# Modulation steps of a decoder trunk's first layer: smaller first blocks, shift and scale side by side, x loaded behind the first steps, and another cost model under the scheduler

## The chip, the cores and the metric

The kernel runs on one core of a Trainium2 chip. The metric is the device time of one execution in microseconds. The kernel before takes 2581.92 us, the median of three runs (2581.72 to 2582.03). The engines named below are TensorE (PE in the profile, its weight loads PEld), VectorE (DVE), ScalarE (ACT), GpSimd (POOL) and SyncE (SP), which issues the kernel's DMAs.

## The reference, cut to what matters

Two layers, 256 tokens, width 2048, FFN width 5632, all in f32:

```python
c_act = silu(c)
for l in range(2):
    mod = c_act @ w_mod[l] + b_mod[l]                  # 2048 x 12288 weights
    shift1, scale1, gate1, shift2, scale2, gate2 = split(mod, 6)
    h = rms_norm(x, norm1_gain[l]) * (1 + scale1) + shift1
    x = x + gate1 * mixer(h, ...)                      # in-projection, three mixers, w_out
    h = rms_norm(x, norm2_gain[l]) * (1 + scale2) + shift2
    x = x + gate2 * (silu(h @ w_gate[l]) * (h @ w_up[l])) @ w_down[l]
return rms_norm(x, final_norm_gain)
```

The mixer projects h with `w_in`, gives its column groups to three token mixers (A: gated linear attention, B: sliding-window attention with rotary positions, C: gated delta rule), concatenates their outputs and projects them with `w_out`. No output of a layer can start before its modulation (`mod`) is there, and `mod` reads 100 MB of weights per layer for a single vector.

## The kernel before, in words

Rows of x are two blocks of 128; the contraction of every projection runs over 16 K tiles of 128. `stream` (from L293) loads one K tile of up to 1024 columns (L323), multiplies it with both row blocks (L358) and gives the finished sums to an evacuation. A weight tile is used either "whole", in one f32 pass, or split into a high part (`wh`, ACT, L330) and a low part (`wl`, DVE, L331) for three faster passes. Layer 0's in-projection and out-projection are whole, all else but a few tiles is split. Loaded tiles live in nine slots (`raw`, `wh`, `wl`).

The modulation is not done on TensorE. `mod_segment` loads rows of `w_mod` (L220) and DVE adds each, times one number of silu(c) per partition, to an accumulator (L223): one **step**. After the 16 K tiles of a segment, `finish` folds the 128 partitions: for shift and scale by four transposes on TensorE (L248) and a sum on DVE (L250, L253, L256), for gates by a product with ones (L238). Layer 0's shift1 and scale1 are cut by K block (`K_BLOCKS`, L37): 512 columns a step, one DMA of 128x512, tiles `g` from an 18-buffer pool. All later segments are 1024 wide, tiles `mraw`, whose pool has two buffers, accumulators `acc`, also two. A queue `mods` holds the steps in the order in which they are wanted; `tick` issues some after each weight tile, by a rate for each stage.

Layer 0's in-projection goes block by block through K: norm the block's columns of x with the shift and scale of that block (L441 to L451), project the groups `qk`, `z`, `v` and `bq` over the block's K tiles, and add the sums to those of earlier blocks on DVE (L969); the first block is copied on ACT (L967). Behind the last block come the keys of B and the delta rule of C (levels at L678, L685 and the transpose L403), then B (L895, L911, L916), the in-projection of A, A itself (L823), the out-projection, norm2 and the FFN. Layer 1 runs the same with one block of all 16 K tiles.

The order in which these calls are written is not the order of the instructions. The framework's scheduler, entered with `tile.TileContext` (L1214), takes the whole program and sets each engine's order by its cost model, keeping the dependences; buffers are then given in that order. SP issues nearly all the kernel's DMAs in one order, and an issue that waits for its buffer holds up all those behind it.

The two places in the code before around the change that the listing does not explain by itself: `K_BLOCKS` is read at L475 to build `mods` and in `layer` to build the blocks, and layer 0 squares x for its norm (L1042) right after it is loaded.

## Time and profile before

| | us |
|---|---|
| median of the runs | 2581.92 |
| profiled execution | 2585.34 |
| its span, first to last instruction | 2583.5 |
| first product of the in-projection | 40.83 |
| last step of the first K block's modulation | 34.92 |

All in all the core moves 600.79 MB at a mean of 233 GB/s; 320 loads of `mraw` are 512 KB each, 128 loads of `g` are 256 KB. The mean granted clock of TensorE is 0.986. In the views below, a window's row gives the stretch, its length, the busy microseconds of PE, PEld, DVE, ACT and POOL with the number of instructions, the granted clock as a share of full speed, the busy share of the 16 DMA engines, and GB/s. A row of the chain gives a start, a duration, the engine and the operation that the end waited for at that time; "issue" is time in which the engine waited for nothing that the profile shows. The page's fifth part and "by line" rows give shares of the span by what the chain was made of.

### The profile page before, as it was taken

The numbers are of one execution on the slowest core, as the hardware profiler recorded it, in microseconds if no ns is written. First come the engines' busy times: TensorE is split into PE (matmuls) and PEld (weight loads), VectorE is DVE, ScalarE is ACT, GpSimd is POOL, SyncE is SP. The second block draws the span as 40 slices with busy tenths as digits, with TensorE's granted clock in tenths as the row PEclk, the third lists the DMA queues.
The fourth block names the chain that finished last, engine by engine and source line by source line (L and its number), as shares of the span: only waits on it lengthen the run. The fifth ranks groups of instructions, "written<-read, shape, count | busy, mean of one in ns | idle before, by whom it ended". The sixth has DMA issues, their size and how long they took to land.

```text
span 2583.5 us, 30803 instructions
## 1 busy us (share of the span) xinstructions
PE 2432.7 (94%) x11164; PEld 1884.1 (73%) x11164; DVE 1714.4 (66%) x2171; ACT 1053.5 (41%) x1548; POOL 58.2 (2%) x117
## 2 busy tenths in 40 slices
PE   4999998889999988999999999999999999999998
PEld 2555785447878767788877878877778878888876
DVE  6767867576675777657578785888664575544555
ACT  2203443124444333344335454564644434344443
POOL 1000000000000000000000000000000000000000
PEclk9999999989999999999999999999999999999999
DMA  9996538777778888868687861675676686666654
GB/s 341 368 322 204 180 114 282 258 231 268 261 259 260 283 268 274 292 193 286 223 277 261 281 192 50 214 232 192 212 256 193 200 286 195 188 191 188 189 184 155
DMA packets 190033, 600.79 MB, mean 233 GB/s; under 512 B 21628, under 2 KB 26268, under 8 KB 189496
## 3 DMA queue, kind: packets, MB, share of 16 engines
q1 hardware_dynamic: 189880, 598.81, 70.7%
q8 instruction: 88, 1.44, 0.2%
q14 instruction: 65, 0.53, 0.1%
HBM read 596.63 MB, written 2.10 MB: 232 GB/s over the span
## 4 chain that ended last, share of the span: by engine, by line
PE 57%; DMA 20%; DVE 10%; issue 8%; ACT 4%; POOL 1%; SPq 1%; DVEq 0%; ACTq 0%; POOLq 0%
PE acc L358 48%; DMA mraw<-in_w_mod 13%; DVE wl L331 4%; DMA raw<-in_w_down 3%; DMA raw<-in_w_in 2%; DVE acc L223 2%; ACT wh L330 1%; PE mm L403 1%; PE ga L895 1%; DMA raw<-in_w_up 1%; PE mm L678 1%; PE mm L685 1%; PE ga L916 1%; DMA raw<-in_w_gate 1%; PE fin L248 1%
## 5 line engine op out<-in xcount | busy, mean ns | idle before, releaser
L358 PE MATMUL acc<-wh,hm 128*128 128x512 f32 (+3 forms) x4872 | 1339.2, 389 | 20.9 <-DVE xs L931 4.7
L330 ACT ACTIVATE wh<-raw 128x1024 fp32r<-128x1024 f32 (+3 forms) x669 | 684.7, 1025 | 985.8 <-PE acc L358 548.9
L331 DVE TENSOR_TENSOR wl<-raw,wh 128x1024 fp32r<-128x1024 f32 (+3 forms) x669 | 785.2, 1179 | 446.6 <-ACT wh L330 444.5
L358 PEld LDWEIGHTS acc<-wh,hm 128*128 128x128 f32 x4872 | 892.0, 189 | 215.8 <-issue 25.5
L358 PE MATMUL acc<-wl,hm 128*128 128x512 f32 (+3 forms) x2484 | 792.3, 394 | 12.2 <-DVE wl L331 9.7
L223 DVE SCALAR_TENSOR_TENSOR acc<-mraw,c_act,acc 128x1024 f32<-128x1024 f32 x320 | 410.3, 1282 | 225.2 <-DMA mraw<-in_w_mod 222.9
L358 PEld LDWEIGHTS acc<-wl,hm 128*128 128x128 f32 x2484 | 458.4, 190 | 124.1 <-DVE wl L331 22.3
L358 PE MATMUL acc<-wh,ahl 128*128 128x512 f32 x560 | 158.4, 397 | 0.0
L358 PEld LDWEIGHTS acc<-wh,ahl 128*128 128x128 f32 x560 | 105.8, 189 | 24.5
L358 PE MATMUL acc<-wl,ahl 128*128 128x512 f32 x280 | 90.8, 398 | 7.2 <-DVE wl L331 7.2
L223 DVE SCALAR_TENSOR_TENSOR g<-g,c_act,g 128x512 f32<-128x512 f32 x128 | 88.7, 747 | 12.6 <-DMA g<-in_w_mod 12.4
L358 PE MATMUL acc<-wh,b 128*128 128x512 f32 (+2 forms) x184 | 74.7, 545 | 2.2 <-ACT b L447 2.1
L358 PE MATMUL acc<-wl,b 128*128 128x512 f32 (+2 forms) x176 | 67.1, 518 | 2.6 <-DVE g L969 2.6
L358 PEld LDWEIGHTS acc<-wl,ahl 128*128 128x128 f32 x280 | 52.2, 189 | 23.1 <-DVE wl L331 11.3
L358 PE MATMUL acc<-raw,b 128*128 128x512 f32 (+2 forms) x176 | 67.6, 524 | 0.0
L358 PEld LDWEIGHTS acc<-wh,b 128*128 128x128 f32 x184 | 35.2, 197 | 30.8 <-issue 23.1
L358 PEld LDWEIGHTS acc<-wl,b 128*128 128x128 f32 x176 | 32.8, 192 | 29.2 <-issue 20.3
L416 ACT ACTIVATE acc<-xs 128x512 f32<-128x512 f32 x32 | 19.0, 595 | 85.7 <-DVE xs L931 85.7
L447 ACT ACTIVATE b<-mm,mod,mod 128x128 f32<-128x128 f32 x24 | 9.2, 461 | 109.7 <-DVE mod L256 92.1
L358 PEld LDWEIGHTS acc<-raw,b 128*128 128x128 f32 x176 | 33.5, 195 | 26.7 <-issue 21.7
L929 DVE TENSOR_TENSOR acc<-acc,gate 128x512 f32<-128x512 f32 x64 | 43.0, 695 | 10.3 <-PE acc L358 10.2
L358 PE MATMUL acc<-raw,hm 128*128 128x512 f32 x88 | 41.7, 598 | 1.4 <-ACT acc L416 1.4
(314 smaller groups left out, 1645.8 us busy)
## 6 DMA issues: line engine op xcount, KB each, us to landing
mraw<-in_w_mod SPq DMA_DIRECT2D x320, 512.0 KB
raw<-in_w_down SPq DMA_DIRECT2D x176, 512.0 KB
raw<-in_w_gate SPq DMA_DIRECT2D x160, 512.0 KB
raw<-in_w_up SPq DMA_DIRECT2D x160, 512.0 KB
raw<-in_w_in SPq DMA_DIRECT2D x72, 512.0 KB
g<-in_w_mod SPq DMA_DIRECT2D x128, 256.0 KB
raw<-in_w_out SPq DMA_DIRECT2D x43, 512.0 KB
raw<-in_w_in SPq DMA_DIRECT2D x32, 264.0 KB
```

The lines of the kernel that those rows point to most:

```text
L223: V.scalar_tensor_tensor(acc, raw[:, a], c_act[:, i + a:i + a + 1], acc, ALU.mult, ALU.add)
L248: TE.transpose(ps[:, i * P:(i + 1) * P], acc[:, (j + i) * P:(j + i + 1) * P], ident)
L330: A.activation(wh[:, :width], raw[:, :width], AF.Copy)
L331: V.tensor_tensor(wl[:, :width], raw[:, :width], wh[:, :width].bitcast(F32), ALU.subtract)
L358: TE.matmul(ps[blk, j][:, :segs[j][2]], xa, parts[j][part], start=i == 0 and n == 0, stop=last and n == len(terms) - 1)
L403: TE.transpose(ps[:, j * P:(j + 1) * P], src[:, j * P:(j + 1) * P], ident)
L416: A.activation(scr[0]() if junk is None else junk, xs[:, blk, j * 512:(j + 1) * 512], AF.Square, accum_out=ssq[blk][:, j:j + 1])
L678: TE.matmul(ps[:, s], LT[blk][:, s], Tm[blk][:, s], start=True, stop=True)
L685: TE.matmul(ps[:, s], U[blk][:, s], m1[:, s], start=True, stop=True)
L895: TE.matmul(ps[:, j * nk:(j + 1) * nk], qT[rows, i + j], kT[rows, g, :nk], start=True, stop=True)
L916: TE.matmul(ps[:, j * 64:(j + 1) * 64], pT[:, j * nk + kb * P:j * nk + (kb + 1) * P], kv[kb][:, P + g * 64:P + (g + 1) * 64], start=kb == ...
L929: V.tensor_tensor(ps, ps, need(gate_row, (l, part, j)), ALU.mult)
```

## The change

It has five parts. `K_BLOCKS` becomes (2, 2, 4, 4, 4). For the two blocks of two K tiles, `first_segment` puts the shift columns and the scale columns side by side: one DMA of 128x2x256, one step, one fold of four transposes for both. x is loaded by row block, each half after four modulation steps, and the constants and norm gains after that (they came first). The small per-layer vectors and the rotary tables move behind the `qk`, `z` and `v` products of the first block. And the scheduler's context is opened with `schedule_with_timeline_sim=True`, so that it ranks instructions by a finer model of the engines; that reorders every engine's instructions from the first to the last.

```diff
--- before.py
+++ after.py
@@ -34,7 +34,7 @@
 FAR = 1.0e30
 
 
-K_BLOCKS = (4, 4, 4, 4)
+K_BLOCKS = (2, 2, 4, 4, 4)
 TAIL_OUT = (3, 6)
 TAIL_FFN = (3, 5)
 LEAD_FFN = (0, 0)
@@ -148,7 +148,6 @@
 
 
     ct = tl(kp, [P, N_FULL], "consts")
-    SY.dma_start(ct, consts[:, :N_FULL])
     n_mask = CONSTS.shape[1] - N_FULL
     masks = tl(kp, [P, n_mask], "masks", BF16)
     c_raw = tl(kp, [P, KD], "c_raw")
@@ -171,32 +170,69 @@
     c_act = tl(kp, [P, KD], "c_act")
     A.activation(c_act, c_raw, AF.Silu)
 
-
...
     trig = {}
...
-    SY.dma_start(xs, x.rearrange("(b p) d -> p b d", p=P))
+
+    def rotary():
+
+        pos_i = tl(kp, [P, NB], "pos_i", I32)
+        SY.dma_start(pos_i, pos)
...
+            trig[name] = r
 
 
     mod_col, gate_row = {}, {}
     SHIFT1, SCALE1, GATE1, SHIFT2, SCALE2, GATE2 = range(6)
+
+    def first_segment(k0):
+
+
+        width = 2 * P
+        st = {}
+
+        def mods_at(w):
+            return w[:, :2 * D].rearrange("p (s n) -> p s n", s=2)[:, :, k0 * P:k0 * P + width]
+
+        def step(i):
+            if i == 0:
+                st["acc"] = scr[1]()
+                G.memset(st["acc"], 0.0)
+                SY.dma_start(st["acc"][0:1].rearrange("p (s n) -> p s n", s=2),
+                             mods_at(b_mod[0:1]))
+            acc = st["acc"]
+            raw = scr[1]()
+            SY.dma_start(raw.rearrange("p (s n) -> p s n", s=2),
+                         mods_at(w_mod[0, i * P:(i + 1) * P]))
+            V.scalar_tensor_tensor(acc, raw, c_act[:, i:i + 1], acc, ALU.mult, ALU.add)
+            if i + 1 == KD:
+                fins.append([FIN_LAG, lambda: finish(acc)])
+
+        def finish(acc):
+            t = tl(smp, [P, 4], f"modfirst{k0}")
+            ps = tl(psf, [P, 512], "fin")
+            for i in range(4):
+                TE.transpose(ps[:, i * P:(i + 1) * P], acc[:, i * P:(i + 1) * P], ident)
+            V.tensor_reduce(t, ps.rearrange("p (a b) -> p a b", a=4), AX.X, ALU.add)
+            V.scalar_tensor_tensor(t[:, 2:], t[:, 2:], 1.0, gains[:, 0, k0:k0 + 2],
+                                   ALU.add, ALU.mult)
+            for j in range(2):
+                mod_col[0, SHIFT1, k0 + j] = t[:, j:j + 1]
+                mod_col[0, SCALE1, k0 + j] = t[:, 2 + j:3 + j]
+
+        return [((0, SHIFT1), lambda i=i: step(i)) for i in range(KD)]
 
     def mod_segment(l, part, k0, nk):
 
@@ -459,7 +495,6 @@
 
     small_t, wgk_t = {}, {}
     gains = tl(kp, [P, DEPTH, 2 * KD], "gains")
-    SY.dma_start(gains, small[:, :, :2 * KD].rearrange("l p n -> p l n"))
 
     def load_small(l):
         small_t[l] = tl(kp, [P, SMALL_W], "small")
@@ -473,8 +508,11 @@
 
     k0 = 0
     for n in K_BLOCKS:
-        for pair in zip(*(mod_segment(0, part, k0, n) for part in (SHIFT1, SCALE1))):
-            mods.extend(pair)
+        if n == 2:
+            mods.extend(first_segment(k0))
+        else:
+            for pair in zip(*(mod_segment(0, part, k0, n) for part in (SHIFT1, SCALE1))):
+                mods.extend(pair)
         k0 += n
     for l in range(DEPTH):
         for parts in ((GATE1,), (SHIFT2, SCALE2), (GATE2,)) if l == 0 else (
@@ -948,7 +986,8 @@
 
     def layer(l):
         wi, wo = w_in[l], w_out[l]
-        load_small(l)
+        if l:
+            load_small(l)
         blocks, at = [], 0
         for n in (K_BLOCKS if l == 0 else (KD,)):
             blocks.append(range(at, at + n))
@@ -1036,6 +1075,14 @@
             gemm(segs, ks, lhs, land(first, last, at), whole=ks if WHOLE_IN[l] else (),
                  lead=ahead(*LEAD_IN) if l and name == "qk" else ())
 
+        if l == 0:
+
+            for blk in range(NB):
+                for _ in range(4):
+                    mods.popleft()[1]()
+                SY.dma_start(xs[:, blk], x[blk * P:(blk + 1) * P])
+            SY.dma_start(ct, consts[:, :N_FULL])
+            SY.dma_start(gains, small[:, :, :2 * KD].rearrange("l p n -> p l n"))
         for blk in range(NB):
             if l == 0:
                 for j in range(4):
@@ -1051,6 +1098,8 @@
             for name in ("qk", "z", "v"):
                 project(name)
             if l == 0 and first:
+                load_small(l)
+                rotary()
                 for o in range(0, n_mask, 512):
                     n = min(512, n_mask - o)
                     t = scr[1]()
@@ -1211,7 +1260,7 @@
         args.append(nc.dram_tensor(f"in_{n}", a.shape, mybir.dt.from_np(a.dtype),
                                    kind="ExternalInput").ap())
     args.append(nc.dram_tensor("out_0", (T, D), F32, kind="ExternalOutput").ap())
-    with tile.TileContext(nc) as tc:
+    with tile.TileContext(nc, schedule_with_timeline_sim=True) as tc:
         trunk(tc, *args)
     r = run_bass_kernel_spmd(nc, [named], core_ids=[0])
     return r.results[0]["out_0"].reshape(1, T, D)
```

The moves, at three places. First SP's order while the second K block's and third K block's modulation is loaded (`g` on a 128x2x256 or 128x512 shape: steps of layer 0's shift and scale; `mraw`: 1024-wide steps, here of gate1; `wh`, `wl`, `raw` from in_w_in: in-projection tiles). Before, at the start of the second block:

```order
L323 DMA wh_347<-in_w_in 128x1024
L213 DMA g_357<-in_b_mod 1x512
L220 DMA g_360<-in_w_mod 128x512
L213 DMA g_363<-in_b_mod 1x512
L220 DMA g_366<-in_w_mod 128x512
L220 DMA g_369<-in_w_mod 128x512
L323 DMA wl_372<-in_w_in 128x1024
L220 DMA g_378<-in_w_mod 128x512
L220 DMA g_381<-in_w_mod 128x512
```

and after the change, in the second block and into the third:

```order
L217 DMA g_281<-in_w_mod 128x2x256
L249 DMA acc_1274<-in_b_mod 1x1024
L256 DMA mraw_1277<-in_w_mod 128x1024
L256 DMA mraw_1286<-in_w_mod 128x1024
L217 DMA g_284<-in_w_mod 128x2x256
```

```order
L256 DMA g_423<-in_w_mod 128x512
L359 DMA wl_566<-in_w_in 128x512
L359 DMA wl_566<-in_w_in 128x256
L359 DMA raw_586<-in_w_in 128x1024
L256 DMA mraw_1311<-in_w_mod 128x1024
L256 DMA mraw_1314<-in_w_mod 128x1024
L256 DMA g_429<-in_w_mod 128x512
L249 DMA g_426<-in_b_mod 1x512
L256 DMA g_442<-in_w_mod 128x512
```

Loads of gate1 rows now stand among the steps of shift and scale, where before none did. Counting bytes down SP's order: the last step of the first block stands at 10.9 MB before and at 8.1 after; of the later blocks, after, at 19.4, 37.0, 52.8 and 64.8.

Second, TensorE's order in layer 0's delta rule (L403, L678 and L685 before are L439, L716 and L723 after; 128x512 rows are products of projections, `ga` rows belong to attention, `fin` to a fold). Before:

```order
L403 MATMUL mm_1713<-consts_88,g_1650 128x128 x4
L678 MATMUL mm_1719<-g_1693,g_1681 128x128 x4
L358 MATMUL acc_2497<-wh_2608,hm_993 128x512
L358 MATMUL acc_2498<-wh_2608,hm_993 128x512
L358 MATMUL acc_2493<-wh_2629,hm_657 128x512
L358 MATMUL acc_2494<-wh_2629,hm_657 128x512
L358 MATMUL acc_2493<-wl_2630,hm_657 128x512
L685 MATMUL mm_1726<-g_1724,g_1690 128x128 x4
L358 MATMUL acc_2494<-wl_2630,hm_657 128x512
```

After:

```order
L954 MATMUL ga_2290<-kv_349,b_2283 128x64
L954 MATMUL ga_2290<-kv_354,b_2283 128x64
L723 MATMUL mm_1769<-g_1767,g_1733 128x128 x4
L933 MATMUL ga_2298<-kT_1468,b_2213 128x256 x2
L439 MATMUL mm_1775<-consts_88,g_1736 128x128 x4
L716 MATMUL mm_1781<-g_1693,g_1681 128x128 x4
L723 MATMUL mm_1788<-g_1786,g_1690 128x128 x4
L949 MATMUL ga_2309<-consts_88,b_2296 128x128 x4
L284 MATMUL fin_3646<-consts_88,acc_3476 128x128 x4
L439 MATMUL mm_1794<-consts_88,g_1693 128x128 x4
L716 MATMUL mm_1800<-g_1736,g_1724 128x128 x4
```

```order
L439 MATMUL mm_1813<-consts_88,g_1736 128x128 x4
L716 MATMUL mm_1819<-g_1693,g_1681 128x128 x4
L439 MATMUL ga_2338<-consts_88,b_120 128x128 x4
L394 MATMUL acc_3457<-wl_3451,hm_1429 128x512
L394 MATMUL acc_3458<-wl_3451,hm_1429 128x512
L394 MATMUL acc_3457<-raw_3467,hm_1429 128x512
```

Before, projection products stand one to four at a time between the steps of each level; after, a level's steps follow one another with attention's between, and the products come in groups of eight.

Third, SP's order where layer 1's in-projection begins. Before:

```order
L220 DMA mraw_11475<-in_w_mod 128x1024
L323 DMA raw_9772<-in_w_in 128x1024
L323 DMA raw_9793<-in_w_in 128x1024
L220 DMA mraw_11514<-in_w_mod 128x1024
L323 DMA raw_9814<-in_w_in 128x1024
L323 DMA raw_9832<-in_w_in 128x1024
L213 DMA acc_11472<-in_b_mod 1x1024
L213 DMA acc_12251<-in_b_mod 1x1024
L220 DMA mraw_11550<-in_w_mod 128x1024
L220 DMA mraw_11571<-in_w_mod 128x1024
L220 DMA mraw_11592<-in_w_mod 128x1024
```

After:

```order
L359 DMA raw_9541<-in_w_down 128x1024
L359 DMA raw_9766<-in_w_in 128x1024
L359 DMA raw_9794<-in_w_in 128x1024
L359 DMA raw_9815<-in_w_in 128x1024
L359 DMA raw_9836<-in_w_in 128x1024
L359 DMA raw_9857<-in_w_in 128x1024
```

Layer 1's in-projection tiles are no longer interleaved with `mraw` loads: from the first in_w_in load of layer 1 to its last in_w_out load there are 64 of these before and none after.

33 lines of the change are left out of this document (15 added, 18 removed).

## The prediction

> **What bounds the kernel now.** I read the engine totals and the chain of the page first, then the first 90 us and the end of layer 0's mixers as a chain of waits in order of time, then the stages as windows.
>
> ```profile
> PE 2432.7 (94%) x11164; PEld 1884.1 (73%) x11164; DVE 1714.4 (66%) x2171; ACT 1053.5 (41%) x1548; POOL 58.2 (2%) x117
> ...
> PE 57%; DMA 20%; DVE 10%; issue 8%; ACT 4%; POOL 1%; SPq 1%; DVEq 0%; ACTq 0%; POOLq 0%
> PE acc L358 48%; DMA mraw<-in_w_mod 13%; DVE wl L331 4%; DMA raw<-in_w_down 3%; DMA raw<-in_w_in 2%; DVE acc L223 2%; ACT wh L330 1%; PE mm L403 1%; PE ga L895 1%; DMA raw<-in_w_up 1%; PE mm L678 1%; PE mm L685 1%; PE ga L916 1%; DMA raw<-in_w_gate 1%; PE fin L248 1%
> ```
>
> TensorE is busy for 2432.7 of 2583.5 us, so 151 us are idle, and no instruction of TensorE goes or comes with this change. It can win back idle time (and a lowered clock behind it) or add some. The largest part of the chain that isn't TensorE is the stream of modulation weights, 13%. Where the idle time lies:
>
> ```profile
> 40.00:220.00 180.00, 175.81 (x529) 97.47 (x530) 125.86 (x218) 29.25 (x66) 2.73 (x16) 0.99 0.95 336
> ...
> 220.00:400.00 180.00, 173.51 (x1032) 137.21 (x1030) 136.71 (x269) 83.98 (x193) 11.72 (x17) 0.96 0.51 160
> 400.00:590.00 190.00, 164.23 (x595) 87.97 (x594) 127.98 (x178) 52.95 (x117) 8.66 (x9) 0.94 0.74 243
> 590.00:980.00 390.00, 373.28 (x1635) 300.04 (x1634) 268.45 (x243) 155.45 (x164) 2.86 (x3) 1.00 0.82 273
> 980.00:1370.00 390.00, 373.69 (x1637) 300.76 (x1636) 260.75 (x254) 156.43 (x175) 4.39 (x6) 0.99 0.78 257
> 1370.00:1600.00 230.00, 221.11 (x1289) 186.10 (x1288) 173.09 (x291) 117.90 (x207) 6.30 (x21) 0.99 0.63 202
> 1600.00:1840.00 240.00, 223.61 (x1240) 180.06 (x1240) 186.61 (x279) 135.69 (x270) 13.91 (x17) 0.98 0.59 190
> 1840.00:2583.00 743.00, 724.07 (x3206) 592.36 (x3204) 408.18 (x387) 310.68 (x336) 1.08 (x2) 0.99 0.65 207
> ```
>
> Columns are stretch, length, busy PE, PEld, DVE, ACT, POOL, clock, DMA share, GB/s. The first 40 us are nearly all idle; the K loop (40 to 220) loses 4; layer 0's mixers 6.5 and then 25.8, with the clock at 0.96 and 0.94 (another 7 + 11 us of full speed); layer 0's FFN 33; layer 1's mixers 8.9 + 16.4, and about 7 by the clock; the rest 19.
>
> **Part 1, the head.** How fast weights arrive, and what the first product waits for:
>
> ```profile
> 0.00:10.00 10.00, 0.00 (x0) 0.00 (x0) 2.18 (x16) 4.69 (x7) 3.59 (x23) 1.00 0.78 267
> 10.00:20.00 10.00, 1.11 (x4) 0.71 (x4) 6.43 (x14) 6.50 (x18) 1.95 (x2) 1.00 0.92 310
> 20.00:30.00 10.00, 0.00 (x0) 0.00 (x0) 9.62 (x15) 0.00 (x0) 0.00 (x0) 1.00 0.99 349
> 30.00:40.00 10.00, 2.23 (x8) 1.43 (x8) 8.51 (x14) 0.00 (x0) 1.05 (x2) 1.00 1.01 372
> ...
> 40.00:80.00 40.00, 39.17 (x115) 22.32 (x116) 27.82 (x45) 10.06 (x24) 1.27 (x2) 1.00 1.02 375
> 80.00:120.00 40.00, 39.22 (x130) 22.10 (x129) 30.75 (x55) 6.22 (x15) 1.46 (x14) 1.00 1.01 361
> ```
>
> ```profile
> 34.92 0.76 DVE g L223
> 35.72 1.13 PE fin L248 x4
> 36.88 0.70 DVE sums L250
> 37.62 1.13 PE fin L248 x4
> ...
> 40.83 2.08 PE acc L358 x2
> ```
>
> By these rates 2.7 MB have come by 10 us, 5.8 by 20, 9.3 by 30, 13.0 by 40, 28.0 by 80. In the order before, 10.9 MB stand up to the 32nd modulation step: 34.3 us by the rates, and the row has its last step at 34.92. So the queue's bytes date the head well. From that step to the first product pass 5.2 us (35.68 to 40.83), with two folds; one fold in place of two saves one pair of rows, 1.8 us, so I take 3.4.
>
> After the change, counted down SP's order in bytes: the last of the 16 side-by-side steps of block 0 stands at 8.1 MB, which is 26.7 us; with the step's 0.7 and the fold's 3.4 the first product starts at 30.8, **10 us earlier**. But a block of two K tiles covers half the time. Sixteen K tiles take 180 us (the window 40 to 220), 11.2 each, so block 0's products end at 53.2. Block 1's last step stands at 19.4 MB, and 13.0 MB at 40 us plus 6.4 at 375 GB/s is 57.1; with the fold it can start at 61.2. **Stall 8 us**, end 83.6. Block 2's last step stands at 37.0 MB: 28.0 at 80 us and 9.0 at 361 GB/s is 104.9; two folds and the norm, 5 us, so it starts at 109.9. **Stall 26 us.** The reason is in the order: 12 loads of gate1 weights (6.3 MB, not needed before layer 0's out-projection) and w_in tiles loaded ahead stand between. Block 3's last step is at 52.8 MB, 149 us, needed at 154.7 less its fold: just in time; block 4's at 64.8 MB, 182, needed at 199. The K loop so ends at 109.9 + 12 x 11.2 = 244 instead of 220: **+24 us**.
>
> Bounds: at 375 GB/s from 40 us on block 2 starts 1 us earlier, and nothing in these rows is faster, so +20 is about the least. And the gate loads use a pool of two buffers: a load waits on SP for the step that frees its buffer, and what is queued behind it (block 2's steps, w_in tiles) isn't issued meanwhile. Before, where nothing else stood between such loads, a pair took 5.4 us:
>
> ```profile
> 178.16 1.30 DVE acc L223
> 179.47 4.00 DMA mraw<-in_w_mod
> 183.52 0.04 issue
> 183.56 1.30 DVE acc L223
> ```
>
> That is 2.5 us more than 1.05 MB at 361 GB/s; six pairs would add 15. As other loads stand between most pairs, I take nothing of it: +24, from +20 to +39.
>
> The Trainium skill ("DMA: Bandwidth & Descriptors", section on bandwidth measured) has 16 MB moving at 425 GB/s for a core that streams alone. At that rate from the first load on, block 1 would start at about 52, block 2 at 95, and the head would cost 9 rather than 24. The rows above, 361 to 375 in stretches where the 16 engines are shown as fully busy, don't reach it, so the sum keeps the rows.
>
> Added work beside it: one more partial sum per column group, about ten adds, as in this row:
>
> ```profile
> 171.74 0.68 DVE g L969
> ```
>
> That is 7 us of DVE, which is idle 12 of 40 us in 40 to 80, and idler still in the stalls; nothing, unless these adds fall between a fold and its block (then 2 to 3 us). Rotary and the small loads go behind block 0's products; they are 0.2 MB, already in the count.
>
> **Part 2, layer 0's mixers.** Before, the modulation for norm2 trails:
>
> ```profile
> 511.26 4.29 DMA mraw<-in_w_mod
> 515.65 1.30 DVE acc L223
> 517.08 1.09 PE fin L248 x4
> ...
> 480.00:520.00 40.00, 34.12 (x84) 15.67 (x83) 19.33 (x19) 0.00 (x0) 0.95 (x1) 0.92 0.78 258
> ...
> 560.00:590.00 30.00, 22.17 (x84) 16.57 (x85) 18.24 (x33) 20.34 (x48) 2.78 (x4) 0.72 0.29 93
> ```
>
> By 480 the fold of shift2 and scale2 sets the end of the chain, with TensorE 5.9 us idle and the clock at 0.92, 9 us in all; 560 to 590 loses 7.8 and 8.4. After the change all of layer 0's steps for norm2 are issued before a third of its w_out loads (134 MB into the queue; before, after the last of them, at 147). So the 9 go, and about a third of the 16, where folds at 571 us stand between norm2 and the first products; TensorE's order there has the same norm. Against it: the levels of the delta rule, a chain through DVE and ACT, now have w_out products in blocks of four or more between them instead of singly, and the last GLA chunks have little beside them. I take **-14**, from -35 (all idle time and half the clock's loss) to +25 (the idle time of 400 to 590 doubled, if the delta rule's levels stand bare).
>
> **Part 3, layer 0's FFN.** Before, 209 MB stand from the first w_gate load to layer 1's first w_in; after, 239 MB: 192 loads of w_mod instead of 135 come here. Over 780 us that is 306 GB/s, where 268 was needed.
>
> ```profile
> 1170.00:1235.00 65.00, 64.98 (x295) 53.63 (x294) 51.11 (x47) 27.07 (x28) 0.00 (x0) 1.00 0.90 302
> 600.00:620.00 20.00, 17.53 (x74) 13.23 (x73) 13.51 (x11) 7.05 (x7) 0.00 (x0) 1.00 0.90 322
> ```
>
> The first row has 302 GB/s with TensorE never idle, the second 322 with 12% idle. DVE takes 57 more steps at the 1.30 us of the rows in part 1, 74 us, on its 529 of 780. I take **0**, between -10 (a third of the idle time) and +30.
>
> **Part 4, layer 1's mixers.** The same loads are missing here: from the first w_in load to the last w_out load SP's order has 90 MB before, 56 after, and 64 loads of w_mod before, none after. The chain of that stretch:
>
> ```profile
> by line: PE acc L358 30.9%; DMA raw<-in_w_in 10.9%; issue 6.8%; DVE wl L331 5.6%; DMA mraw<-in_w_mod 3.3%; ACT wh L330 3.0%; PE ga L895 2.7%; DMA raw<-in_w_out 2.2%; PE mm L685 2.1%; PE mm L678 2.1%; PE ga L916 2.1%; PE mm L403 1.5%; DVE ac
> ```
>
> Of 470 us the chain waits 16 for w_mod and 51 for w_in, and DVE gets 83 of its 360 us free (64 steps of 1.30) for the splits and the mixers' short steps. What can be won is the 25 us of idle time and 7 of the clock: **-20**, from 0 to -32. Layer 1's FFN has 32 loads of w_mod before and after, 0.
>
> **Sum.** 24 - 14 + 0 - 20 = -10. The profiled execution has a span of 2583.5 and a time of 2585.3, the median of the runs is 2581.9; taken off the median, 2572.
>
> **Rivals.**
>
> *The FFN is bound by its loads (slower).* Place: layer 0's FFN up to the 95th w_gate load, 212 MB after against 180, about 670 us by its share of the bytes, so 316 GB/s. It decides from the point where the loads, which wait on SP for the slot that the split frees, keep under that. At the 302 of the row above the stretch takes 702, 30 us more, and DVE at 77% delays splits. 24 - 14 + 30 - 20 = +20: 2602. For it: the row with 322 loses 12%. Against it: in the K loop 361 to 375 run beside a TensorE that is 98% busy.
>
> *All cancels.* The gains later are only what the head costs, -24 in parts 2 and 4 by their smaller ends and a few us in part 3: 2582, no difference.
>
> *The order fills the gaps far better.* Parts 2 and 4 reach their ends: 24 - 35 - 32 = -43: 2539. For it: 50 us of loss in 220 to 590. Against it: much of that is the serial norm2 and the delta rule, whose steps are unchanged.
>
> *The head costs little.* Block 2's 37.0 MB are there at 90 us, not 105, so its stall falls by 15 and the head costs +9: the sum is -25, 2557. That needs 411 GB/s on the mean, where the rows of the first 40 us show 267 to 372 and the next ones 375 and 361; for it speaks only that the DMA share of the first two rows, 0.78 and 0.92, leaves room.
>
> This is the case that the Trainium skill's 425 GB/s would make likeliest; the rows here speak against it.
>
> **How the numbers follow.** Forecast 0.40 (2553 to 2577 its own range), FFN bound 0.36, cancelling 0.13, far better 0.07, cheap head 0.04. Within 0.2%, which is 5 us and about what can be told from no change: 0.13. Faster 0.40 + 0.07 + 0.04 = 0.51, slower 0.36. The range takes in most of the slow case (up to +38) and of the good one: 2527 to 2620.
>
> **What would show it.** First TensorE product near 31 us, gaps in TensorE of about 8 us near 53 and 26 near 84, the K loop over near 244; no wait of a fold for w_mod before norm2; DMA over 300 GB/s through layer 0's FFN with TensorE at 96% or more (below, the slow rival); no w_mod load in layer 1's mixers and TensorE over 97% busy there. I am wrong if the stall at 84 is missing, or if 220 to 590 gets longer than its 370 us.

## The result, and the profile after

The changed kernel takes 2713.15 us, the kernel before beside it 2581.82: a ratio of 1.0513, with a 95% interval of 1.0494 to 1.0531. It is 131 us slower. The profiled execution has a span of 2710.4 us against 2583.5. The engine totals of the page and the clock row of the changed kernel:

```profile
PE 2479.7 (91%) x11164; PEld 1938.8 (72%) x11164; DVE 1727.4 (64%) x2193; ACT 1060.2 (39%) x1554; POOL 54.4 (2%) x117
...
PEclk9799999879999999999999999988899999999999
```

The instructions of TensorE are the same 11164. Its idle time rose from 151 us to 231, and its busy time by 47, and the granted clock fell (mean 0.957 against 0.986). Matmuls behind a gap run longer: four products of one shape take 3.78 us at 164.01 in the timeline below, right behind a gap, and 1.88 at 170.06, at full clock again. Stage by stage, from the windows of the additions of K blocks, of the FFN's gate evacuations and of the gated additions to x, each to 2 us:

| stage | before | after | difference |
|---|---|---|---|
| to the last K block's last addition | 240 | 266 | +26 |
| layer 0's mixers and out-projection | 322 | 370 | +48 |
| norm2 to the first gate chunk | 62 | 52 | -10 |
| layer 0's FFN | 744 | 774 | +30 |
| layer 1's mixers and out-projection | 452 | 468 | +16 |
| norm2 of layer 1 to its first gate chunk | 48 | 50 | +2 |
| layer 1's FFN to its last addition | 706 | 720 | +14 |

The sum is +126, the two spans differ by 127. No stage is to blame alone; the change lost time in every stage but one. (The expectations quoted below cut the stages a little wider, from the first instruction that belongs to the next one: 415, 795 and 500 us there are 370, 774 and 468 here.) Windows of the changed kernel (columns as before), with the stages' own bounds:

```profile
266.00:636.00 370.00, 317.92 (x1489) 223.57 (x1487) 225.03 (x374) 119.57 (x263) 16.40 (x22) 0.90 0.53 169
...
688.00:1462.00 774.00, 722.13 (x3160) 583.87 (x3159) 584.59 (x550) 302.60 (x329) 12.01 (x13) 0.98 0.86 295
1462.00:1930.00 468.00, 436.95 (x2415) 366.90 (x2414) 271.13 (x477) 234.02 (x430) 11.64 (x31) 0.95 0.41 122
```

and of the kernel before:

```profile
240.00:562.00 322.00, 295.64 (x1477) 198.74 (x1475) 228.83 (x370) 107.57 (x246) 17.00 (x21) 0.97 0.65 211
...
624.00:1368.00 744.00, 714.27 (x3128) 575.07 (x3126) 502.06 (x471) 298.53 (x322) 7.23 (x8) 0.99 0.80 263
1368.00:1820.00 452.00, 429.16 (x2472) 354.54 (x2473) 351.99 (x562) 241.12 (x450) 18.95 (x36) 0.99 0.62 200
```

Layer 0's mixers have 52 us of idle time instead of 26, at a clock of 0.90. Layer 1's have 31 instead of 23, though DVE has 81 us less to do there and the loads fell from 200 to 122 GB/s: less traffic, and still slower.

The first two gaps of the head came close to the forecast, and a third that it didn't have. TensorE's timeline after the change:

```profile
52.78 1.02 PE L394 MATMUL acc<-wl,b 128*128 128x512 f32 x2
57.20 0.66 PE L227 MATMUL fin<-consts,g 128*128 128x128 f32 x4 [3.40 <-DVE g L219]
59.33 3.50 PE L394 MATMUL acc<-raw,b 128*128 128x512 f32 x4 [1.47 <-ACT b L483]
...
82.77 1.02 PE L394 MATMUL acc<-wh,b 128*128 128x512 f32 x2
101.84 1.11 PE L284 MATMUL fin<-consts,g 128*128 128x128 f32 x4 [18.05 <-DVE g L259]
...
108.68 3.78 PE L394 MATMUL acc<-wl,b 128*128 128x512 f32 x4 [3.83 <-ACT b L483]
...
155.14 2.74 PE L394 MATMUL acc<-wl,b 128*128 128x512 f32 x6
...
164.01 3.78 PE L394 MATMUL acc<-raw,b 128*128 128x512 f32 x4 [2.62 <-ACT b L483]
...
170.06 1.88 PE L394 MATMUL acc<-wl,b 128*128 128x512 f32 x4
```

From 53.8 to 59.3 and from 83.8 to 108.7 there is no product: 5.5 and 24.9 us, where 8 and 26 were forecast. Each waits for a fold, and the fold for the last step on DVE. At the fourth block, called just in time in the forecast, there is none from 157.9 to 164.0, 6.1 us.

### The profile page after: what moved, and what is told of

Its sections match the earlier page's. It is cut to its first block, busy times and chain, and to the rows that moved or that the text cites. A ratio compares the mean times of both kernels' runs of the same rounds, so it can differ in the third digit from the quotient of the medians.

```text
span 2710.4 us, 30972 instructions
## 1 busy us (share of the span) xinstructions
PE 2479.7 (91%) x11164; PEld 1938.8 (72%) x11164; DVE 1727.4 (64%) x2193; ACT 1060.2 (39%) x1554; POOL 54.4 (2%) x117
## 4 chain that ended last, share of the span: by engine, by line
PE 42%; DMA 9%; DVE 6%; ACT 3%; issue 2%; POOL 0%; SPq 0%; ACTq 0%; DVEq 0%; POOLq 0%
PE acc L394 38%; DMA mraw<-in_w_mod 5%; DVE wl L367 2%; DVE acc L259 2%; ACT wh L366 1%; DMA raw<-in_w_up 1%; DMA raw<-in_w_gate 1%; DMA raw<-in_w_down 1%; DVE acc L967 1%; PE mm L439 0%; DMA raw<-in_w_in 0%; PE ga L933 0%; DMA raw<-in_w_out 0%; PE ga L954 0%; PE ga L439 0%
## 5 line engine op out<-in xcount | busy, mean ns | idle before, releaser
L394 PE MATMUL acc<-wh,hm 128*128 128x512 f32 (+3 forms) x4872 | 1354.4, 391 | 28.7 <-DVE xs L969 17.6
L394 PEld LDWEIGHTS acc<-wh,hm 128*128 128x128 f32 x4872 | 903.7, 191 | 229.5 <-issue 39.5
L394 PE MATMUL acc<-wl,hm 128*128 128x512 f32 (+3 forms) x2484 | 808.0, 395 | 10.7 <-DVE wl L367 9.5
L259 DVE SCALAR_TENSOR_TENSOR acc<-mraw,c_act,acc 128x1024 f32<-128x1024 f32 x320 | 410.2, 1282 | 157.9 <-DMA mraw<-in_w_mod 155.9
L394 PE MATMUL acc<-raw,b 128*128 128x512 f32 (+2 forms) x176 | 76.1, 537 | 4.1 <-ACT b L483 4.1
L394 PE MATMUL acc<-wl,b 128*128 128x512 f32 (+2 forms) x176 | 74.5, 528 | 4.4 <-ACT b L483 4.4
L259 DVE SCALAR_TENSOR_TENSOR g<-g,c_act,g 128x512 f32<-128x512 f32 x96 | 68.0, 745 | 1.3 <-DMA g<-in_w_mod 1.3
L394 PEld LDWEIGHTS acc<-raw,b 128*128 128x128 f32 x176 | 34.3, 199 | 32.7 <-issue 24.8
L969 DVE TENSOR_TENSOR xs<-xs,acc 128x512 f32<-128x512 f32 x64 | 41.7, 680 | 0.3
```

The lines of the kernel that those rows point to most:

```text
L259: V.scalar_tensor_tensor(acc, raw[:, a], c_act[:, i + a:i + a + 1], acc, ALU.mult, ALU.add)
L394: TE.matmul(ps[blk, j][:, :segs[j][2]], xa, parts[j][part], start=i == 0 and n == 0, stop=last and n == len(terms) - 1)
L969: V.tensor_tensor(x_j, x_j, ps, ALU.add)
```

## The experiments

### Which part of the change costs the time

Four kernels: the finer model alone on the kernel before; the change without it; the change with the old blocks; and the change with neither.

```diff
-    with tile.TileContext(nc) as tc:
+    with tile.TileContext(nc, schedule_with_timeline_sim=True) as tc:      # flag_only, on before
```
```diff
-    with tile.TileContext(nc, schedule_with_timeline_sim=True) as tc:
+    with tile.TileContext(nc) as tc:                                       # no_flag, on after
```
```diff
-K_BLOCKS = (2, 2, 4, 4, 4)
+K_BLOCKS = (4, 4, 4, 4)                    # flag_4444, on after; no_flag_4444, on no_flag
```

> The kernel before with nothing changed but the scheduler's finer model. Theory S (the reordering is the cost: of the 127 us between the two profiles, 28 lie up to the end of the K loop, 37 in layer 0's mixers, 28 in layer 0's FFN, 22 in layer 1's mixers, 12 in layer 1's FFN, and only the first 28 have to do with the K blocks): 2660 to 2710 us, with the losses behind the K loop as in the changed kernel. Rival K (the K blocks and the moved loads are the cost, the rest follows from modulation steps that they displace): under 2610.

> The changed kernel (K blocks 2,2,4,4,4, side by side, x behind the first steps, rotary and small loads moved) under the scheduler's old model. Theory S: 2570 to 2590 us; the first product near 31 us instead of 40.8, a gap of at most 8 us at the second block, none at the third since no gate1 rows stand before it. Rival K: 2610 or more, with the gap at the third block as long as in the changed kernel, 21 us.

> The changed kernel with K blocks 4,4,4,4 again, the finer model kept. Theory S: 2670 to 2710 us, since the finer model still runs gate1 steps ahead and the parts behind the K loop are ordered by it. Rival K: under 2620.

> The old model and K blocks 4,4,4,4: only the x, constant, gain, small and rotary loads are moved. The bytes ahead of the first block's last step are the same but for 0.4 MB of small loads and constants, so both theories expect the time of before within 5 us, 2577 to 2587, and the first product at 39 to 42 us.

Measured: the finer model alone 2722.41 us, ratio 1.0544 (1.0508 to 1.0580); the change without it 2587.29, 1.0018 (0.9998 to 1.0038); the finer model with the old blocks 2712.98, 1.0513 (1.0479 to 1.0546); neither 2582.71, 1.0010 (0.9994 to 1.0027). So the reordering is the whole loss, and what was written into the program by hand is worth nothing that these runs can tell. The two kernels with the finer model lie a little above what was expected of them (2710 at most); the other two lie inside. The stages of the finer model alone differ from those of the changed kernel by 7 us at most.

Why the hand-written part gains nothing, although it works: without the finer model the first product starts 12 us earlier than before, at 28.96 against 40.83, and yet the K loop's last addition is no earlier. Timeline of TensorE in the change without the finer model, and its window at the third block:

```profile
26.12 1.11 PE L227 MATMUL fin<-consts,g 128*128 128x128 f32 x4 [6.88 <-DVE g L219]
...
28.96 6.12 PE L394 MATMUL acc<-wh,b 128*128 128x512 f32 x8
...
80.00:90.00 10.00, 2.35 (x9) 1.55 (x9) 8.99 (x17) 0.63 (x2) 1.05 (x2) 0.59 0.79 248
```

The additions of the K blocks, before and there (first and last start are the two numbers joined by "to"):

```profile
L969 DVE TENSOR_TENSOR b<-b,acc x12: 677/681/689, 136.2 to 240.1; 128x512 f32<-128x512 f32 x12
```
```profile
L1008 DVE TENSOR_TENSOR b<-b,acc x16: 676/680/690, 77.2 to 242.1; 128x512 f32<-128x512 f32 x16
```

240.1 and 242.1. Starting sooner only brings TensorE sooner to weights that aren't there yet: it is idle for 7.7 us at the third block instead, and no product runs from 79.7 to 89.9, 10.2 us. No gap at the third block was expected there, so that point was a miss. From 90 us to the end of the K loop TensorE is idle for 3.5 us only. What sets the end is not settled: the DMA engines are full for most of the first 150 us (a share of 0.92 or more in 14 of 15 windows of 10 us before, of 0.99 or more in 10 of 15 here), and no run tested the bytes by themselves.

### The gate steps in the head

The changed kernel, with gate1's steps held: the first two loads of each of its segments wait for a column of the last block's normed x.

```diff
+            elif (l, part) in pin and i < 2 * rows:
+                G.tensor_copy(raw[:, 0:1], pin[l, part])
...
+            if last and not l:
+                pin[l, GATE1] = h[1][3][0][:, 0, 0:1]
```

> The changed kernel with layer 0's gate1 steps made to wait for the last K block's norm. The last steps of blocks 1 and 2 then stand at 16.9 and 30.6 MB instead of 19.4 and 37.0. Theory E (the gap of 25 us at the third block is the gate1 loads ahead of its steps): that gap falls under 10 us, the one at the second under 3, the K loop ends 15 to 22 us earlier: 2690 to 2700 in all. Rival (what the head wins, the mixers lose, since the gate steps come later): 2708 or more.

Measured: 2702.39 us, ratio 1.0484 (1.0415 to 1.0553). The total is too near to the changed kernel's to count on; the profile is clear.

```profile
83.78 1.02 PE L397 MATMUL acc<-wh,b 128*128 128x512 f32 x2
90.42 1.12 PE L286 MATMUL fin<-consts,g 128*128 128x128 f32 x4 [5.62 <-DVE g L261]
...
96.20 3.54 PE L397 MATMUL acc<-wl,b 128*128 128x512 f32 x4 [2.76 <-ACT b L486]
```

The gap at the third block is 11.4 us instead of 24.9 (under 10 was expected), and the one at the second 3.9 instead of 5.5 (under 3 was expected). So the gate loads make up 13.5 us of the long gap; the other 11.4 are near the 10.2 that the kernel without the finer model has there, where no gate loads stand in between. The K loop ends at 246 instead of 266, and 10 of these 20 us are lost again in layer 0's mixers, 380 instead of 370.

### Layer 1's steps in layer 0's FFN

The changed kernel, with layer 1's shift2, scale2 and gates held until layer 1's first norm, by the same copy:

```diff
+            if last and l:
+                for part in (SHIFT2, SCALE2, GATE1, GATE2):
+                    pin[l, part] = h[1][0][1][:, 0, 0:1].bitcast(F32)
```

> The changed kernel with layer 1's shift2, scale2 and gate steps made to wait for layer 1's first norm, so that they can't run ahead into layer 0's FFN: 189 MB are issued between its first gate load and layer 1's first in-projection load instead of 239. Theory D (layer 0's FFN is held by its loads, 28 us of the 127): the FFN goes from 795 to about 767 us, layer 1 within 10 of its 500: 2675 to 2700. Rival (the FFN is held by the order of its transposes behind DVE's short steps, whatever the loads): the FFN stays at 785 or more, and the time at 2700 or more.

Measured: 2733.75 us, ratio 1.0605 (1.0533 to 1.0678), the range of neither theory in both points: the FFN falls as theory D had it, the total rises as the rival had it. Its two stages, and the busy time of the projections' products alone (L397 in this kernel) in two stretches of 20 us of the second:

```profile
694.00:1436.00 742.00, 711.83 (x3117) 581.00 (x3115) 462.47 (x438) 298.00 (x321) 6.28 (x7) 0.98 0.73 240
1436.00:1952.00 516.00, 457.53 (x2451) 377.36 (x2452) 386.77 (x589) 239.31 (x438) 27.91 (x49) 0.94 0.63 209
```
```profile
1710.00:1730.00 20.00, 0.00 (x0) 0.66 0.74 237
...
1790.00:1810.00 20.00, 0.00 (x0) 0.81 0.00 1
```

The FFN is back at 742 us, where it was before (744), with 189 MB of loads instead of the 209 there: so its 30 us are the steps that were moved into it, by the wait for loads or on DVE. What takes their place is dearer: layer 1's mixers, now with 96 loads of `w_mod`, go from 468 to 516. The kernel before has 64 loads in this stage and takes 452. But the order has changed with the hold as well: from 1710 to 1810, five such stretches in a row, no product of a projection runs. So how much of the 48 us is the steps themselves, and how much the order around them, is not shown.

### What holds the mixers

Three cuts, each on both kernels: four of six loop levels of the delta rule; half of attention's units; and 12 of 16 steps of layer 0's gate1, shift2 and scale2 (whose folds then also follow the last step at once, where they waited for some four more weight tiles). Each cut kernel is scheduled anew, so the order of what is left differs too.

```diff
-        for m in LEVELS[1:]:
+        for m in LEVELS[5:]:                                               # levels_*
```
```diff
+        G.memset(o[:, :, 1], 0.0)
...
-            for r in range(2):
+            for r in range(1):                                             # attn_half_*
```
```diff
+        at = range(0, KD, rows)
+        if few:                                    # layer 0's gate1, shift2, scale2
+            at = (0, 5, 10, 15)
-        return [((l, part), lambda i=i: step(i)) for i in range(0, KD, rows)]
+        return [((l, part), lambda i=i: step(i)) for i in at]              # mods_few_*
```

> The kernel before without four of the delta rule's six loop levels (2, 4, 8, 16 left out; the delta rule's result is no longer exact). 16 level steps in two layers go, each some 2.6 us of TensorE. Theory C (before, projection products stand between the level steps and cover them; in the changed order the levels are bare): only TensorE's own work is saved here, 30 to 50 us: 2530 to 2555. Rival (the chain is as bare before as after): 75 us or more saved, 2505 or less.

> The changed kernel without the same four levels. Theory C: the level steps follow each other at about 7 us (375 to 460 us for twelve), so that 16 of them are worth 80 to 110 us: 2605 to 2635. Rival (they are covered here too, and the mixers lose elsewhere): 30 to 50 us saved, 2663 to 2683.

> The kernel before with half of sliding-window attention left out (one of two heads of each pair; its part of the output is zero): 12 of 24 score units, each some 4.3 us of TensorE. Theory A (before, the units' links through DVE and ACT are covered by products): 35 to 60 us saved, 2520 to 2547. Rival (the units' latency sets the mixers' time here too): 80 or more saved, under 2500.

> The changed kernel with the same half of attention left out. Leaving out the delta rule's levels saved 3 us only, so it isn't they that set the mixers' time. Theory A (attention's units do: they share one PSUM bank, so one follows the other, 13 to 14 us apart in layer 1, 24 of them): 90 to 150 us saved, 2563 to 2623. Rival (something else in the mixers): 35 to 60 us saved or less, 2653 or more.

> The kernel before with 12 of 16 steps left out of each 1024-wide segment of layer 0's gate1, shift2 and scale2 (72 loads, 38 MB, 92 us of DVE; the modulation is not the reference's). Both theories: the wait for w_mod before norm2 goes, 10 to 30 us saved, 2552 to 2572.

> The changed kernel with the same 72 steps left out. Theory M (in the changed order the steps stand on DVE between the links of attention and wait there for their loads, so that attention goes at the pace of the loads in layer 0): 35 to 65 us saved, 2648 to 2678, with layer 0's mixers at 385 us or less instead of 415. Rival (the units are spread by the products that stand between their links on TensorE): 10 to 25 us saved, all of it in the K loop and before norm2, 2688 to 2703.

> The kernel before with both cuts, half of attention and four of six delta rule levels left out. From the last addition of layer 0's FFN to the last of layer 1's out-projection it takes 455 us whole, 440 without the levels, 445 without half of attention. Both theories: the cuts add up, 425 to 435, and 2515 to 2530 in all.

> The changed kernel with both cuts. The same stretch of layer 1 takes 470 us whole, 470 without the levels, 460 without half of attention. Theory P (in layer 1 the two chains stand side by side without products beside them, so that either alone holds the time): with both cut 440 or less, and with a further gain of 5 to 20 in layer 0, where the modulation steps hold the time, 2655 to 2680 in all. Rival (neither chain holds it, the order of products and projections behind them does): 455 or more, 2685 or more in all.

| left out | total before, us | total after, us | layer 0 mixers, before / after | layer 1 mixers, before / after |
|---|---|---|---|---|
| nothing | 2581.82 | 2713.15 | 322 / 370 | 452 / 468 |
| levels | 2540.07 | 2709.86 | 308 / 362 | 440 / 470 |
| half of attention | 2563.70 | 2700.53 | 314 / 364 | 444 / 460 |
| both | 2525.56 | 2610.54 | 292 / 314 | 426 / 422 |
| layer 0's steps | 2568.33 | 2664.01 | 296 / 332 | 454 / 470 |

(The ratios to the kernel before, with their intervals, in the order of the table: 0.9854, 0.9784 to 0.9924, and 1.0513, 1.0442 to 1.0584; 0.9934, 0.9913 to 0.9955, and 1.0454, 1.0331 to 1.0576; 0.9779, 0.9674 to 0.9885, and 1.0109, 1.0018 to 1.0199; 0.9951, 0.9933 to 0.9969, and 1.0312, 1.0190 to 1.0435. In the kernel before without layer 0's steps the K loop ended 22 us later than in the kernel before, so for it the end of layer 0's out-projection counts: 558 instead of 562, against 588 instead of 636 in the changed order.)

Before, the cuts about add up: 12 and 8 us in layer 1, 26 with both. After, the levels alone give nothing and half of attention 8, but both give 46, and layer 1 is then as fast as before the change with the same cuts (422 against 426). My theory that the levels hold the mixers fell with its run, and the one after it, that attention does, fell with the next; half of attention also gave the kernel before less, 18 us, than either theory had. As far as these runs show, what holds them is the two chains side by side: with one cut, the stage keeps most of its time. For both cuts theory P was right on layer 1 (440 or less), but layer 0 gained 56 us where 5 to 20 were expected, so the total, 2610.54, lies far below the 2655 expected at the least.

What fits this is where the projections' products stand. Time of the products alone, in 20 us, before the change in layer 0 and layer 1 (the poorest rows of 280 to 560 and 1540 to 1800), as windows of that line:

```profile
320.00:340.00 20.00, 6.82 (x22) 1.00 0.11 28
...
1580.00:1600.00 20.00, 6.10 (x20) 1.00 0.18 53
```

and after it:

```profile
420.00:440.00 20.00, 0.00 (x0) 1.00 0.59 179
...
460.00:480.00 20.00, 0.00 (x0) 0.76 0.67 192
...
580.00:600.00 20.00, 0.00 (x0) 0.50 0.00 1
...
1740.00:1760.00 20.00, 0.00 (x0) 1.00 0.00 1
1760.00:1780.00 20.00, 0.00 (x0) 0.81 0.00 1
```

(The columns are stretch, length, the products' busy time and count, clock, DMA share, GB/s.) Before, no 20 us of the mixers are without 6 us of products; after, there are five such stretches with none at all, and the clock falls to 0.50 in one. In three of them hardly a load moves either.

It is not that the chains have fewer products beside them on the whole. Layer 1's levels are twelve steps, each begun by the product L716 (L678 before). TensorE's rows of some of them, after the change:

```profile
1712.84 1.06 PE L716 MATMUL mm<-g,g 128*128 128x128 f32 x8
...
1721.87 1.06 PE L716 MATMUL mm<-g,g 128*128 128x128 f32 x8
...
1743.01 1.06 PE L716 MATMUL mm<-g,g 128*128 128x128 f32 x8
...
1747.28 1.06 PE L716 MATMUL mm<-g,g 128*128 128x128 f32 x8
```

Before, the trace has 62 products between the first and the last of these steps, at most 6 in one place, and a step every 4.1 to 5.7 us. After, it has 186 (many of them narrower), 13 to 25 in one place, all ahead of the sixth step, and none behind it. The early steps come 8.6 to 9.1 us apart, as from 1712.84 to 1721.87, and the bare late ones 2.8 to 6.3, most of them no slower than before, as from 1743.01 to 1747.28. So bare steps aren't long in themselves; the products are spent on the early ones, and beside the late ones TensorE has only the chains' own short products.

In layer 0 there is a second thing: modulation steps stand on DVE between the links of the chains, and wait there for their own loads. DVE's timeline after the change:

```profile
449.24 1.28 DVE L259 SCALAR_TENSOR_TENSOR acc<-mraw,c_act,acc 128x1024 f32<-128x1024 f32 x1 [1.60 <-DMA mraw<-in_w_mod]
452.06 1.28 DVE L259 SCALAR_TENSOR_TENSOR acc<-mraw,c_act,acc 128x1024 f32<-128x1024 f32 x1 [1.54 <-DMA mraw<-in_w_mod]
453.26 0.68 DVE L286 TENSOR_REDUCE sums<-fin 128x4 f32<-128x512 f32 x1
454.88 1.28 DVE L259 SCALAR_TENSOR_TENSOR acc<-mraw,c_act,acc 128x1024 f32<-128x1024 f32 x1 [0.94 <-DMA mraw<-in_w_mod]
456.08 0.68 DVE L724 TENSOR_TENSOR g<-g,mm 128x512 f32<-128x512 f32 x1
456.68 0.68 DVE L936 TENSOR_TENSOR b<-ga,masks 128x512 f32<-128x512 f32 x1
```

TensorE's rows of the same time:

```profile
449.24 1.06 PE L723 MATMUL mm<-g,g 128*128 128x128 f32 x8
450.23 1.13 PE L933 MATMUL ga<-kT,b 64*128 64x256 f32 x4
454.00 0.66 PE L284 MATMUL fin<-consts,acc 128*128 128x128 f32 x4 [2.65 <-DVE sums L286]
456.82 1.12 PE L439 MATMUL mm<-consts,g 128*128 128x128 f32 x4 [2.16 <-DVE g L724]
```

The level's product (L723) was issued on TensorE at 449.24 and took 1.06 us; its subtraction (L724) stands behind three steps and a fold and comes at 456.08. Attention's mask (L936) waits in the same line: its scores were issued at 450.23, and DVE takes them at 456.68. The level's next transpose (L439) waits for DVE until 456.82. With 72 steps left out, layer 0's mixers go from 370 to 332, so they are worth 38 us there, where 48 were lost; leaving out parts of both chains gives 56. The two act on the same time and can't be added.

### Products put back between the levels

If the chains only lack products, putting some back should help. A's in-projection was made to wait, in both layers, for a tile that the delta rule makes right before its levels; the trace then has 404 and 384 products between the first and the last step of the levels of layer 0 and layer 1, where it had 36 and 186. (The counts in the expectations below, some 290 against 18 and 96, are lower than those of the traces.)

```diff
             LT[blk] = lt
+            after_lt[:] = [lt[:, 0:1]]
...
+            if wait is not None:                   # each weight load of A's projections
+                G.tensor_copy(raw[:, 0:1], wait)
```

> The changed kernel with the weight loads of A's in-projection made to wait for a tile that the delta rule makes right before its levels, in both layers. TensorE's order then has some 290 products between the first and the last level of each layer, where the changed kernel has 18 and 96. Theory P (the two chains run out of products): layer 1 from the end of layer 0's FFN to its out-projection falls from 468 to 435 to 455, layer 0 from the K loop's end to its out-projection from 370 to 320 to 350: 2650 to 2685 in all. Rival (the chains cost their time wherever the products stand, or A's loads come too late): 2700 or more.

> The same with layer 0's gate1 steps made to wait for the last K block's norm as well. If what the two holds win adds up, the K loop ends near 246 instead of 266 and the time is 10 to 20 us below that of the first hold alone; if the gate steps then stand in the way of the chains, it is the same or above.

> The kernel before with the same wait of A's weight loads. Its order has 74 and 62 products between the levels and 220 and 210 between the first and last attention unit, and no 20 us without products. Theory P: nothing to win, 2575 to 2600, more likely above 2582 since A's products come later. Rival: faster than 2575.

Measured: 2758.64 us, ratio 1.0677 (1.0641 to 1.0714); with gate1 held too 2734.51, 1.0583 (1.0549 to 1.0618); on the kernel before 2612.70, 1.0118 (1.0092 to 1.0145). A miss for the theory as I had put it, and for the rival a hit (2700 or more): the hold costs time in both orders. Layer 0's mixers take 400 us instead of 370, layer 1's 478 instead of 468. The products' windows in the first of them show where it went:

```profile
280.00:300.00 20.00, 0.00 (x0) 0.50 0.66 197
300.00:320.00 20.00, 0.00 (x0) 0.50 0.66 187
320.00:340.00 20.00, 0.00 (x0) 0.51 0.66 189
340.00:360.00 20.00, 0.00 (x0) 0.83 0.73 228
```

The 80 us ahead of the levels (convolution, norms, first attention units) are now without products, three quarters of them at half clock, and so are the last chunks of mixer A from 600 to 620. My reading is that there is one stock of products for the whole chain of mixers: bunched anywhere, they leave it bare elsewhere. That an even spread would bring the changed order to the time before is not shown, since no run made one. The two holds did add up: gate1's is worth 24 us here (10 to 20 were expected), and the K loop ends at 246 again.

No kernel that computes the whole was faster than the kernel before beyond its interval.

## Why the prediction was wrong

The forecast was 2572, faster; the time is 2713, outside the range. It is also outside what the sum's own terms allowed: their upper ends, 39, 25, 30 and 0, add up to 2676, which the range cut off at 2620. Two steps failed, both on the mixers. Step by step:

- *The head, +24.* The size came, +25 (last addition at 265.4 instead of 240.1), and the bytes counted down SP's order, at rates from the trace, dated the folds to 2 us: first product 29.0 (30.8 forecast), stalls 5.5 and 24.9 us (8 and 26). Half of the second stall's cause is shown too: holding the gate steps took 13.5 us off it. But the sum was lucky. It took the K loop before to end at 220, 11.2 us for a K tile, though its last addition is at 240.1, 12.5 a tile (block 0 took 24.8 us for two). With 12.5 the same dates give stalls of 5.4 and 23.7, nearer still, but a sum of +19. The 6 that are missing are the third stall, from 157.9 to 164.0, which the sum had as just in time.
- *Layer 0's mixers, "I take -14, from -35 ... to +25".* Wrong: +48, and -10 for norm2. The folds of shift2 and scale2 no longer trail (the last run at 492 to 496), as the sum had it, though norm2 is as short in the change without the finer model, 51 us. The step that failed is the rest: I saw in the order that the levels stood bare, priced it as a bound and gave it nothing in the middle value. I also looked at the delta rule alone; attention's chain runs beside it, and with either one cut the stage keeps 362 or 364 of its 370 us, with both cut 314. And of the steps that were moved ahead I counted the bytes, but not that each can stand in DVE's queue in front of a link of the chains: without 72 of them the stage takes 332.
- *Layer 0's FFN, 0 from -10 to +30.* At the end of its bound: +30. The row with 322 GB/s and 12% idle that I quoted for the rival was the better guide than the K loop's rows: the stage has 295 GB/s with TensorE 93% busy, below the 96% that the forecast had named as the sign of this rival. Held back, the steps gave all 30 us back. This rival had its place and price right (30 us), and its total, 2602, wrong, since it took the two gains for granted. Whether its cause, the loads, was right too, or the steps' work on DVE costs the time, is not shown.
- *Layer 1's mixers, "What can be won is the 25 us of idle time and 7 of the clock: -20, from 0 to -32".* The step that failed worst: it went to +16, outside a bound for which I gave no reason. I read the idle time as a wait for loads and for DVE, because the chain of waits named w_in and w_mod, and put what the new order of TensorE would cost here at nothing. With 64 loads and 81 us of DVE less the stage got slower: idle time 31 us instead of 23 and a clock of 0.95 instead of 0.99. The new order spends its products on the early steps and has none at 1740 to 1780, with 150 us of the stage to go. What the missing loads gave by themselves isn't shown, since no run took them out in the old order.
- *Layer 1's FFN, 0.* +14, not foreseen and not settled. Products wait 10.9 us for their accumulators there instead of 3.0, which is 8 of the 14; no run tested it.
- *The rivals.* None had this mechanism. All kept the gains of parts 2 and 4, so they differed only in how much a loss elsewhere took back. "The order fills the gaps far better" is what a finer model promises; the opposite case, that it spends its filler early, was missing from the list.
- *What the Trainium skill would make of the head.* The Trainium skill ("DMA: Bandwidth & Descriptors", section on bandwidth measured) has 425 GB/s for one core alone. The changed head shows 383 to 398 GB/s in the rows from 50 to 100 us, where the kernel before has 389 at most in its first 150 us, and not 425; the stalls came as the rows had them, so the measured rows decide here.

The highest of these rows, as a window of the changed kernel:

```profile
60.00:70.00 10.00, 10.00 (x26) 5.19 (x25) 8.82 (x13) 0.93 (x3) 0.00 (x0) 0.88 1.04 398
```

## What to carry to other kernels

When a change reorders a whole program, split it first: one run with the ordering alone and one with the hand-written part alone told more here than every estimate of stages. Fewer loads and less work on another engine did not make a stage with two long serial chains faster once its order had changed: ask how many independent products stand beside each step of the chains and where they run out, and read that as the products' own busy time in equal slices, where one empty slice says more than any mean. When two chains run side by side, cut them together as well as one at a time. Give a bound on the wrong side to every gain whose cause is only a name in the chain of waits.

## What the runs showed of the hardware

Pieces of 1 KB, for shift and scale side by side, moved a little more slowly than pieces of 2 KB. The changed kernel has 381 GB/s at 10 to 20 us and 357 at 20 to 30, with the DMA engines at a busy share of 1.06 and 1.08:

```profile
10.00:20.00 10.00, 0.66 (x2) 0.29 (x2) 6.71 (x13) 3.85 (x9) 2.18 (x3) 1.00 1.06 381
20.00:30.00 10.00, 2.58 (x8) 1.66 (x9) 5.96 (x12) 1.85 (x6) 0.00 (x0) 1.00 1.08 357
...
100.00:110.00 10.00, 3.55 (x10) 2.23 (x11) 9.45 (x16) 1.80 (x5) 0.00 (x0) 0.50 1.04 386
```

The same kernel with the old blocks (the finer model kept) has 392 and 394, at a share of 1.04:

```profile
10.00:20.00 10.00, 1.09 (x4) 0.72 (x4) 6.42 (x13) 3.85 (x9) 1.79 (x2) 1.00 1.04 392
20.00:30.00 10.00, 0.00 (x0) 0.00 (x0) 2.85 (x4) 0.00 (x0) 0.10 (x1) 1.00 1.04 394
```

The 310 and 349 of the kernel before come with 2 KB pieces too, but in another order of loads.

A gap of TensorE cost more than its length: with no work from 83.8 to 101.8 us its granted clock stood at 0.50 in 90 to 100, and in the window 100 to 110 too, when products had begun again. The first four products behind it took 3.78 us, and four of the same shape 1.88 at 170.06, where the clock is 1.00 again. Over the whole kernel the idle time grew by 80 us and the span by 127; the other 47 are the same 11164 matmuls taking longer, which fits the lower clock.
